# Starting every SBUF tile of a two-layer decoder trunk on a multiple of 256 bytes

## The chip, the cores and the metric

The kernel runs on one core of one Trainium2 chip. Times are device microseconds of one execution of the whole program; the number compared is the median of several executions. Before the change three executions gave 946.52, 948.52 and 952.02 us, median 948.52 us.

TensorE (PE) multiplies a stationary operand of at most 128x128 with a moving operand of up to 512 columns and writes to PSUM. The load of the stationary operand is an instruction of its own in the trace, LDWEIGHTS, shown as engine PEld. VectorE (DVE), ScalarE (ACT) and GpSimd (POOL) do the elementwise work, and SyncE (SP) issues every DMA here. SBUF has 128 partitions; an address below is a byte offset inside a partition, the same in all of them.

## The reference

A causal trunk of two layers on 512 tokens of 1024 features, all in float32:

```
for i in range(2):
    hn = rms_norm(h, norm_mix[i])
    h += pooling_mixer(hn)  if i == 0  else  sliding_window_attention(hn)
    hn = rms_norm(h, norm_ffn[i])
    u = hn @ w_in                      # 1024 -> 2 * 2816
    c = causal_depthwise_conv(u, width 3) + conv_b
    a, g = split(c)
    h += (a * silu(g)) @ w_out         # 2816 -> 1024
out = rms_norm(h, norm_f)
```

The pooling mixer takes windowed means (2, 4, 8, 16 tokens) minus the token and multiplies each group of 256 features with its own matrix. The attention has 16 query heads on 4 key heads, a window of 128, a bias by distance and one sink per head.

## The kernel before

Activations lie feature-major, 128 features by 512 tokens in a tile of 2048 bytes per partition. A float32 product is made of three passes: each operand is split into a high and a low float32r part, and `mm3` (lines 78 to 82) issues high x high, low x high and high x low, with a weight slice of 128 columns stationary and the activations moving. So nearly all of PE's work is a stream of matmuls with 512 moving columns, each with its own weight load.

In order of time:

- Pooling mixer, line 252: `xt` against the band matrices (line 267), then `px` parts against `wpool` parts, 48 matmuls.
- MLP of layer 0, lines 371 to 375: twice a half of the input projection (`mlp_in`, `f0x` parts against `wi` parts, 528 matmuls a half) and of the output projection (`mlp_out`, `zh`/`zl` against `wo`, 264 matmuls a half).
- Attention, lines 378 to 617: keys and queries (`ax` against `kq`), values (`wv` moving, `ax` stationary, 256 columns), then 16 units of scores (`kh`/`kl` against `q`, line 536), softmax, transposes (line 567) and weighted values (`th`/`tl` against `vh`/`vl`, 256 columns) with query and output projections filled in between, and the rest of the output projection (`oh`/`ol` against `wo`).
- MLP of layer 1, lines 621 to 657, as in layer 0 with `f1x`. The last output projection runs five of its eight chunks with 512 columns; the last three are done in two halves of 256 columns, one of them with its weights in the tiles named `wk`.

Weights come by DMA into `raw` tiles (line 86), ACT copies the high part (line 94) and DVE or POOL subtracts for the low part (line 95), a few tiles ahead of PE. The order on each engine is the order of the code, held together by semaphores.

Where a tile lies follows from the pools. Pools stand one behind the other in SBUF, and each tile in them takes its size rounded up to 32 bytes. A tile of one column takes 32 bytes, and everything behind it is shifted by that. The pool `cst` stands first, then `wp` (weights), `xp` (`h` and the parts of the normed activations), `sm` (small and shared tiles), and behind them one pool for each phase: `first`, `fp0`, `ap`, `fp1`.

Of the kernel before, what the change touches and what calls it, by code (L numbers as in the profile page):

```python
"""Two-layer hybrid decoder trunk (pooling mixer, sliding-window attention, gated conv MLPs).

Activations are kept feature-major, [feature (partition), chunk, token], so that every product has
a weight tile as its stationary and all 512 tokens as its moving operand, and the causal
convolution runs along the free dimension.

float32 products: each operand is split exactly into two float32r parts, x = h + l, and a product
is the three passes hh + hl + lh. The scale of an RMSNorm is per token: it is multiplied in after
the product that follows the norm.
"""  # L10
# [9 lines left out]
F32 = mybir.dt.float32  # L20
F32R = mybir.dt.float32r
I32 = mybir.dt.int32
AF = mybir.ActivationFunctionType
# [3 lines left out]
P = 128  # L27
D = 1024
S = 512
NC = D // P  # feature chunks  # L30
NT = S // P  # token tiles
WINDOWS = (2, 4, 8, 16)
BW = P + 16  # tokens that a token tile's windows reach
FF = 2816
NF = FF // P  # chunks of one half of the MLP's input projection
NFH = NF // 2
HD = 64
# [5 lines left out]
# Columns of the packed per-feature vectors.  # L43
# [10 lines left out]
NV = V_SINK + NH  # L54
# [3 lines left out]
def trunk(ctx: ExitStack, tc: tile.TileContext, x_tok, x_t, vecs, w_pool, w_kq, w_v, w_o, w_in, w_out, out_a, out_b):  # L58
# [9 lines left out]
    # The banks of PSUM, handed out round-robin within rings that each phase sets.  # L68
    pp = ctx.enter_context(tc.tile_pool(name="pp", bufs=1, space=PSUM))
    banks = [pp.tile([P, S], F32, name=f"bank{i}") for i in range(8)]  # L70
    rings = {}
# [17 lines left out]
    def weights(src, n, name, eng=None, raw=None):  # L89
        """[128, n] of a weight from DRAM, n <= 1024, as its two parts."""  # L90
        raw = raw or fetch(src, n, name)
        h = wp.tile([P, 1024], F32R, tag="wh", name=f"{name}_h")
        l = wp.tile([P, 1024], F32R, tag="wl", name=f"{name}_l")
        A.activation(h[:, :n], raw[:, :n], AF.Copy)  # L94
        (eng or V).tensor_tensor(l[:, :n], raw[:, :n], h[:, :n].bitcast(F32), ALU.subtract)  # L95
        return h, l
# [14 lines left out]
    def kept_weights(layer, half, m):  # L111
        """The same, in the tiles of the split activations, which are free by then."""
        res = []
        for a in range(0, NFH, 4):
            n = (min(a + 4, NFH) - a) * P
            raw = fetch(w_out[layer, half, m, :, a * P : a * P + n], n, f"wk{m}_{a}")
            h = xp.tile([P, S], F32R, tag="xh", name=f"wk{m}_{a}_h")
            l = xp.tile([P, S], F32R, tag="xl", name=f"wk{m}_{a}_l")
            A.activation(h[:, :n], raw[:, :n], AF.Copy)
            V.tensor_tensor(l[:, :n], raw[:, :n], h[:, :n].bitcast(F32), ALU.subtract)  # L120
            res += [part((h, l), k) for k in range(n // P)]
        return res

    eps = cst.tile([P, 1], F32, name="eps")
    V.memset(eps, EPS)

    def load_root(x, name):
        """Has the scalar engine load the square root's table ahead of its use."""
        A.activation(sm.tile([P, 1], F32, tag="root", name=name), x, AF.Sqrt)
# [9 lines left out]
    vec = cst.tile([P, NV], F32, name="vec")  # L139
# [13 lines left out]
    # Windowed mean minus identity, as [token, token it reaches], for inner tiles and the first.  # L153
    rc = fst.tile([P, 16], F32, name="rc")
# [18 lines left out]
    def rsqrt_mean(dst, ssq, n, root=False):  # L173
        """dst = (ssq / D + eps) ** -0.5 on [128, n], from an integer guess or from the scalar engine's square root."""

        def tmp(k, dt=F32):
            return sm.tile([P, NT], dt, tag=f"rs_{k}", name=f"rs_{k}", bufs=4)[:, :n]

        v = tmp("v")
        y = tmp("y")  # L180
        if root:
            A.activation(y, ssq, AF.Sqrt, bias=eps, scale=1.0 / D)
            V.tensor_scalar(v, ssq, -0.5 / D, -0.5 * EPS, ALU.mult, ALU.add)
            V.reciprocal(y, y)
        else:
            V.tensor_scalar(v, ssq, 1.0 / D, EPS, ALU.mult, ALU.add)
            sh = tmp("i", I32)
            V.tensor_scalar(sh, v.bitcast(I32), 1, None, ALU.logical_shift_right)
            V.tensor_scalar(y.bitcast(I32), sh, -1.0, float(0x5F3759DF), ALU.mult, ALU.add)
            V.tensor_scalar(v, v, -0.5, None, ALU.mult)  # L190
        t = tmp("t")
        steps = 1 if root else 3
        for it in range(steps):
            z = dst if it == steps - 1 else y
            if n == 1:
                V.scalar_tensor_tensor(t, y, y, v, ALU.mult, ALU.mult)
            else:
                V.tensor_tensor(t, y, y, ALU.mult)
                V.tensor_tensor(t, t, v, ALU.mult)
            V.scalar_tensor_tensor(z, t, 1.5, y, ALU.add, ALU.mult)  # L200

    class Norm:
        """Sums of squares of the chunks of h, then the scale of each token."""
# [17 lines left out]

        def stats(self, ps, tiles=range(NT)):
            """r[token, tile]."""
            n = len(tiles)
            for i, j in enumerate(tiles):
                T.matmul(ps[:, 2 * i : 2 * i + 2], lhsT=self.acc[:, j * P : (j + 1) * P], rhs=ones[:, :2], start=True, stop=True)  # L226
            r = sm.tile([P, NT], F32, tag="r", name=f"{self.name}_r")
            rsqrt_mean(r[:, :n], ps[:, : 2 * n].rearrange("p (a b) -> p a b", b=2)[:, :, 0], n)
            return r

        def spread(self, ps, r, tiles=range(NT)):
            """r broadcast over the partitions, [128, token]."""
# [10 lines left out]
    def split_scaled(src, g, name):  # L243
        """The parts of src * g, g per feature."""
        xh = xp.tile([P, S], F32R, tag="xh", name=f"{name}_h")
        xl = xp.tile([P, S], F32R, tag="xl", name=f"{name}_l")
        A.activation(xh, src, AF.Copy, scale=g)  # L247
        V.scalar_tensor_tensor(xl, src, g, xh.bitcast(F32), ALU.mult, ALU.subtract)  # L248
        return xh, xl

    # ================= layer 0: pooling mixer =================
    def pool_mixer(norm, xs, ws):
        r0 = fst.tile([P, NT], F32, name="r0")
        ss0 = fst.tile([P, NT], F32, name="ss0")
                # The tensor engine's clock rises only after some microseconds of products.
        warm = fst.tile([P, BW], F32, name="warm")
# [35 lines left out]
        bs = cst.tile([P, NC], F32, name="bs")  # L292
# [12 lines left out]
    # ================= gated MLP with causal depthwise convolution =================  # L305
    def conv_chunk(fp, layer, ps, rb, m, name):
        """The convolution of chunk m of the input projection."""
# [9 lines left out]
    def mlp_in(fp, layer, half, xs, norm, rb, ws0=None):  # L317
        """Half of the hidden features, as chunks of parts. Without rb, the norm is finished on the way."""
# [58 lines left out]
    # ================= layer 1: sliding-window attention =================  # L377
    rings.update(t=[6, 7], s=[2, 3, 4], pj=[5, 0], av=[1])
    with tc.tile_pool(name="ap", bufs=2) as ap:
        # dist[q, j] = j - 128 - q for key j of [previous block, block], where query q sees it.  # L380
# [4 lines left out]
        # Queries are scaled by HD**-0.5 / slope, and the scores with their distances by slope.  # L385
        slopes = [2.0 ** (-8.0 / NH * (i + 1)) for i in range(NH)]
        qs = ap.tile([P, NC], F32, name="qs", bufs=1)
        for i in range(NH):
            G.memset(qs[(i % 2) * HD : (i % 2 + 1) * HD, i // 2 : i // 2 + 1], HD**-0.5 / slopes[i])
        bqs = ap.tile([P, NC], F32, name="bqs", bufs=1)  # L390
        V.tensor_tensor(bqs, vec[:, V_BQKV : V_BQKV + 8], qs, ALU.mult)

        # Values, [token, zero | head 0 | zero | head 1 | ... | zero].
# [11 lines left out]
        # Keys and values.  # L405
# [25 lines left out]
        def keys(n):  # L431
            """The parts of a head's keys, each in both halves of the partitions."""
# [11 lines left out]
        def queries(c, ps):  # L444
            """Per head of a chunk of queries, its high part in its half of the partitions and its low part in the other."""
# [26 lines left out]
        # Work for the tensor engine between the stages of the attention.  # L472
# [24 lines left out]
        def work():  # L497
            """Yields after each step, once its operands are there, the units of attention that the next one needs."""
# [22 lines left out]
        def scores(n, b):  # L521
            w = P if b == 0 else 2 * P
            neg = ap.tile([P, 4], F32, tag="neg", name=f"neg{n}{b}", bufs=3)
            den = ap.tile([P, 4], F32, tag="den", name=f"den{n}{b}", bufs=3)
            es = ap.tile([P, 4], F32, tag="es", name=f"es{n}{b}", bufs=3)
# [63 lines left out]
        # A unit's scores, the transposes of the one two before, and the values of the one three before.  # L589
        RATE = 3.4  # steps of filling work per unit  # L590
# [28 lines left out]
    # ================= layer 1: MLP, then the last norm =================  # L619
    HS = S // 2  # L620
    with tc.tile_pool(name="fp1", bufs=2) as fp:
# [19 lines left out]
        def turn(m):  # L641
            """The second half of the tokens of a chunk, token-major."""
# [46 lines left out]
        r = sm.tile([P, NT], F32, tag="r", name="n3b_r")  # L689
# [72 lines left out]
```

## Time and profile before

| | |
|---|---|
| three executions | 946.52, 948.52, 952.02 us |
| span of the profiled execution | 950.6 us (the page gives no other time of it) |
| PE busy | 929.2 us, 98% |
| PEld busy | 775.0 us, 82% |
| DVE busy | 586.8 us, 62% |
| ACT busy | 426.6 us, 45% |
| POOL busy | 139.2 us, 15% |
| DMA, mean over the span | 93 GB/s |

A matmul is shown for longer than it keeps the next one off: the matmuls overlap in PE's pipeline, and each one's end is modelled. What a matmul costs in a stream is the distance between its start and the next one's, and that is read from the start times or from the count of matmuls in a stretch. A stretch counts every matmul that is shown in it, so also the one or two (0.39 us shown, one started every 0.23 us, so 1.7 on average) that had started before it.

### The profile page before, as it was taken

The numbers are of one execution on the slowest core, as the hardware profiler recorded it, in microseconds if no ns is written. First come the engines' busy times: TensorE is split into PE (matmuls) and PEld (weight loads), VectorE is DVE, ScalarE is ACT, GpSimd is POOL, SyncE is SP. The second block draws the span as 40 slices with busy tenths as digits, with TensorE's granted clock in tenths as the row PEclk, the third lists the DMA queues.
The fourth block names the chain that finished last, engine by engine and source line by source line (L and its number), as shares of the span: only waits on it lengthen the run. The fifth ranks groups of instructions, "written<-read, shape, count | busy, mean of one in ns | idle before, by whom it ended". The sixth has DMA issues, their size and how long they took to land.

```text
span 950.6 us, 11713 instructions
## 1 busy us (share of the span) xinstructions
PE 929.2 (98%) x4419; PEld 775.0 (82%) x4419; DVE 586.8 (62%) x974; ACT 426.6 (45%) x690; POOL 139.2 (15%) x203
## 2 busy tenths in 40 slices
PE   8999999999999999997999999999999999999997
PEld 7788888888888888885788888888888888888886
DVE  5689675336777654338888571897753367776433
ACT  7565443223444433226877551644432234444432
POOL 9500000000000001442654231000000000000013
PEclk9999999999999999997999999999999999999998
DMA  8133323332322233322101031332223332222322
GB/s 328 64 111 114 108 62 81 101 131 93 110 89 86 71 92 106 111 89 67 45 23 46 1 133 45 111 125 97 70 83 92 132 100 101 89 97 62 91 61 89
DMA packets 28855, 88.13 MB, mean 93 GB/s; under 512 B 3200, under 2 KB 4352, under 8 KB 28800
## 3 DMA queue, kind: packets, MB, share of 16 engines
q1 hardware_dynamic: 28800, 87.40, 28.3%
q8 instruction: 34, 0.56, 0.2%
q14 instruction: 21, 0.17, 0.1%
HBM read 85.29 MB, written 2.10 MB: 92 GB/s over the span
## 4 chain that ended last, share of the span: by engine, by line
PE 90%; DVE 5%; ACT 3%; POOL 1%; issue 1%; ACTq 0%; DVEq 0%; POOLq 0%
PE bank L80 29%; PE bank L81 29%; PE bank L82 29%; PE bank L536 1%; DVE q L455 1%; PE bank L567 1%; ACT sc L555 1%; DVE sc L539 1%; ACT px_h L247 0%; DVE tl L571 0%; DVE vl L468 0%; ACT wi_h L94 0%; PE bank L267 0%; DVE f0x_l L248 0%; PE bank L226 0%
## 5 line engine op out<-in xcount | busy, mean ns | idle before, releaser
L220 POOL TENSOR_TENSOR n_acc<-n_acc,n_sq 128x512 f32<-128x512 f32 (+1 forms) x28 | 39.6, 1414 | 720.4 <-ACT n_sq L211 713.6
L94 ACT ACTIVATE wi_h<-wi_raw 128x1024 fp32r<-128x1024 f32 x88 | 93.0, 1061 | 111.0 <-PE bank L81 101.8
L80 PE MATMUL bank<-zh,wo_h 128*128 128x512 f32 (+1 forms) x363 | 138.9, 383 | 0.0
L82 PE MATMUL bank<-zh,wo_l 128*128 128x512 f32 (+1 forms) x363 | 138.4, 381 | 0.0
L81 PE MATMUL bank<-zl,wo_h 128*128 128x512 f32 (+1 forms) x363 | 138.4, 381 | 0.0
L81 PE MATMUL bank<-f0x_l,wi_h 128*128 128x512 f32 x352 | 137.1, 389 | 0.5 <-DVE f0x_l L248 0.5
L80 PE MATMUL bank<-f0x_h,wi_h 128*128 128x512 f32 x352 | 137.2, 390 | 0.0
L80 PE MATMUL bank<-f1x_h,wi_h 128*128 128x512 f32 x352 | 137.1, 390 | 0.0
L82 PE MATMUL bank<-f0x_h,wi_l 128*128 128x512 f32 x352 | 137.0, 389 | 0.0
L82 PE MATMUL bank<-f1x_h,wi_l 128*128 128x512 f32 x352 | 137.0, 389 | 0.0
L81 PE MATMUL bank<-f1x_l,wi_h 128*128 128x512 f32 x352 | 136.9, 389 | 0.0
L95 DVE TENSOR_TENSOR wi_l<-wi_raw,wi_h 128x1024 fp32r<-128x1024 f32 x84 | 102.6, 1224 | 49.7 <-ACT wi_h L94 37.9
L94 ACT ACTIVATE wo_h<-wo_raw 128x768 fp32r<-128x768 f32 (+1 forms) x70 | 57.5, 823 | 129.4 <-PE bank L81 116.9
L309 DVE TENSOR_TENSOR c_u<-bank,n_rb 128x512 f32<-128x512 f32 x88 | 60.0, 687 | 75.6 <-PE bank L82 75.6
L95 DVE TENSOR_TENSOR wo_l<-wo_raw,wo_h 128x768 fp32r<-128x768 f32 (+1 forms) x66 | 60.4, 914 | 56.3 <-ACT wo_h L94 56.1
L82 PEld LDWEIGHTS bank<-zh,wo_l 128*128 128x128 f32 x363 | 68.2, 188 | 14.5
L81 PEld LDWEIGHTS bank<-zl,wo_h 128*128 128x128 f32 x363 | 68.2, 188 | 14.3
L80 PEld LDWEIGHTS bank<-zh,wo_h 128*128 128x128 f32 x363 | 68.2, 188 | 14.3
L81 PEld LDWEIGHTS bank<-f0x_l,wi_h 128*128 128x128 f32 x352 | 66.1, 188 | 14.4 <-DVE f0x_l L248 1.0
L80 PEld LDWEIGHTS bank<-f0x_h,wi_h 128*128 128x128 f32 x352 | 66.1, 188 | 14.1 <-DVE h L301 0.4
L312 ACT ACTIVATE c_t<-c_u,vec 128x512 f32<-128x512 f32 x88 | 70.6, 811 | 15.4 <-DVE c_u L309 14.5
L82 PEld LDWEIGHTS bank<-f1x_h,wi_l 128*128 128x128 f32 x352 | 66.1, 188 | 13.8
(173 smaller groups left out, 1515.9 us busy)
## 6 DMA issues: line engine op xcount, KB each, us to landing
wi_raw<-w_in SPq DMA_DIRECT2D x88, 512.0 KB, 3.2
wo_raw<-w_out SPq DMA_DIRECT2D x31, 384.0 KB, 3.1
wo_raw<-w_out SPq DMA_DIRECT2D x31, 320.0 KB, 2.9
kq_raw<-w_kq SPq DMA_DIRECT2D x10, 512.0 KB, 3.3
wo_raw<-w_o SPq DMA_DIRECT2D x8, 512.0 KB, 3.2
xt<-x_tok SPq DMA_DIRECT2D x4, 512.0 KB, 5.2
h<-x_t SPq DMA_DIRECT2D x8, 256.0 KB, 8.1
wpool_raw<-w_pool SPq DMA_DIRECT2D x2, 512.0 KB, 7.9
```

The costliest lines, as they stand in the source:

```text
L80: T.matmul(ps, lhsT=wh, rhs=xh, start=start, stop=False, **kw)
L81: T.matmul(ps, lhsT=wh, rhs=xl, start=False, stop=False, **kw)
L82: T.matmul(ps, lhsT=wl, rhs=xh, start=False, stop=stop, **kw)
L94: A.activation(h[:, :n], raw[:, :n], AF.Copy)
L95: (eng or V).tensor_tensor(l[:, :n], raw[:, :n], h[:, :n].bitcast(F32), ALU.subtract)
L220: eng.tensor_tensor(self.acc[:, lo:hi], self.acc[:, lo:hi], sq[:, lo:hi], ALU.add)
L309: V.tensor_tensor(u, ps, rb, ALU.mult)
L312: A.activation(t, u, AF.Identity, bias=col(V_CB + layer * 2 * NF + m), scale=cw[2])
L455: V.tensor_tensor(t[dst], u[src], t[src].bitcast(F32), ALU.subtract)
L536: T.matmul(o, lhsT=qt, rhs=kt[:, kk : kk + 256], start=x == 0, stop=x == 1)
L539: V.tensor_tensor_reduce(out=st[:, par, :w], in0=ps[:, par * 256 : par * 256 + w], in1=dist[:, 2 * P - w :], scale=slopes[4 * n + i], scal ...
L555: A.activation(t, t, AF.Exp, bias=neg[:, i : i + 1], accum_out=den[:, i : i + 1])
```

## The change

A helper `small` asks the pool for a tile of a given number of 32-bit words and returns its first columns. It is used for all tiles that are not already a multiple of 256 bytes, with sizes chosen so that the tiles behind them begin on a multiple of 256 bytes. Comments and docstrings are emptied, which shifts line numbers by a few. No instruction is added, taken away or moved on any engine, and no wait changes; operands keep their shapes. What differs is the address of nearly every tile. The end of the used SBUF moves from byte 226,176 to byte 228,096.

```
+    def small(pool, n, words, dt=F32, **kw):
+        return pool.tile([P, words], dt, **kw)[:, :n]
...
-    eps = cst.tile([P, 1], F32, name="eps")
+    eps = small(cst, 1, 32, name="eps")
...
-        A.activation(sm.tile([P, 1], F32, tag="root", name=name), x, AF.Sqrt)
+        A.activation(small(sm, 1, 32, tag="root", name=name), x, AF.Sqrt)
...
-    vec = cst.tile([P, NV], F32, name="vec")
+    vec = small(cst, NV, -(-NV // 64) * 64, name="vec")
...
-    rc = fst.tile([P, 16], F32, name="rc")
+    rc = small(fst, 16, 64, name="rc")
...
-            return sm.tile([P, NT], dt, tag=f"rs_{k}", name=f"rs_{k}", bufs=4)[:, :n]
+            return small(sm, n, 16, dt, tag=f"rs_{k}", name=f"rs_{k}", bufs=4)
...
-            r = sm.tile([P, NT], F32, tag="r", name=f"{self.name}_r")
+            r = small(sm, NT, 32, tag="r", name=f"{self.name}_r")
...
-        warm = fst.tile([P, BW], F32, name="warm")
+        warm = small(fst, BW, 192, name="warm")
...
-        bs = cst.tile([P, NC], F32, name="bs")
+        bs = small(cst, NC, 64, name="bs")
...
-        qs = ap.tile([P, NC], F32, name="qs", bufs=1)
+        qs = small(ap, NC, 32, name="qs", bufs=1)
...
-            neg = ap.tile([P, 4], F32, tag="neg", name=f"neg{n}{b}", bufs=3)
-            den = ap.tile([P, 4], F32, tag="den", name=f"den{n}{b}", bufs=3)
-            es = ap.tile([P, 4], F32, tag="es", name=f"es{n}{b}", bufs=3)
+            neg = small(ap, 4, 32, tag="neg", name=f"neg{n}{b}", bufs=3)
+            den = small(ap, 4, 16, tag="den", name=f"den{n}{b}", bufs=3)
+            es = small(ap, 4, 16, tag="es", name=f"es{n}{b}", bufs=3)
```

(`r0`, `ss0`, `bqs` and the last `r` are changed in the same way.)

The remainders of the tiles' addresses, as the two programs are built. The slices that PE takes of a float32r tile begin a multiple of 256 bytes into it, so a slice has its tile's remainder.

| tiles | address mod 256 before | after |
|---|---|---|
| weights in `wp` (`wi`, `wo`, `kq`, `wv`: raw, h, l) | 160 | 0 |
| `xp`: `h`, `px`, `f0x`, `ax`, `f1x`, `wk` | 160 | 0 |
| `zh`, `zl`, `c_u`, `c_t`, `zz`, `hg`, `xt` | 32 | 0 |
| `wpool` parts | 224 | 0 |
| `oh`, `ol`, `kh`, `kl`, `q`, `vh`, `vl`, `n_acc`, `n_sq` | 96 | 0 |
| `sc`, `th`, `tl`, `ident`, `ones` | 128 | 0 |

So before the change the two operands of a matmul have these remainders (moving, stationary): `f0x`, `f1x` and `ax` against `wi` and `kq` 160 and 160; `wv` against `ax` 160 and 160; `kh`, `kl` against `q` 96 and 96; `zh`, `zl` against `wo` or `wk` 32 and 160; `oh`, `ol` against `wo` 96 and 160; `px` against `wpool` 160 and 224; `th`, `tl` against `vh`, `vl` 128 and 96. After it all of them have 0 and 0.

## Rows read from the trace of the kernel before

**Rows 1.** The page: span, busy time of the engines, chain that ended last.
```profile
span 950.6 us, 11713 instructions
PE 929.2 (98%) x4419; PEld 775.0 (82%) x4419; DVE 586.8 (62%) x974; ACT 426.6 (45%) x690; POOL 139.2 (15%) x203
PE 90%; DVE 5%; ACT 3%; POOL 1%; issue 1%; ACTq 0%; DVEq 0%; POOLq 0%
```

**Rows 2.** Stretches: start:end, length, PE busy, instructions, granted clock, DMA.
```profile
60.00:150.00 90.00, 90.00 (x399) 1.00 0.29 94
152.00:212.00 60.00, 60.00 (x259) 1.00 0.34 105
334.00:393.00 59.00, 59.00 (x255) 1.00 0.35 106
440.00:480.00 40.00, 35.61 (x199) 0.91 0.16 54
480.00:520.00 40.00, 37.06 (x231) 0.96 0.11 40
```

**Rows 3.** Timeline of PE, input projection: start, shown length, engine, line, operands.
```profile
99.96 0.39 PE L80 MATMUL bank<-f0x_h,wi_h 128*128 128x512 f32 x1
...
102.91 0.39 PE L81 MATMUL bank<-f0x_l,wi_h 128*128 128x512 f32 x1
```

**Rows 4.** Timeline of PE, output projection of the MLP.
```profile
160.06 0.39 PE L80 MATMUL bank<-zh,wo_h 128*128 128x512 f32 x1
...
162.86 0.39 PE L80 MATMUL bank<-zh,wo_h 128*128 128x512 f32 x1
```

**Rows 5.** Timeline of PE, end of the attention's output projection.
```profile
570.17 0.39 PE L80 MATMUL bank<-oh,wo_h 128*128 128x512 f32 x1
...
574.84 0.39 PE L82 MATMUL bank<-oh,wo_l 128*128 128x512 f32 x1
```

**Rows 6.** Timeline of PE, products of the pooling mixer.
```profile
19.98 0.40 PE L80 MATMUL bank<-px_h,wpool_h 128*128 128x512 f32 x1
...
23.94 0.39 PE L82 MATMUL bank<-px_h,wpool_l 128*128 128x512 f32 x1
```

**Rows 7.** Timeline of PE, matmuls of 256 columns: values, then last output projection.
```profile
409.77 0.28 PE L80 MATMUL bank<-wv_h,ax_h 128*128 128x256 f32 x1
...
411.69 0.28 PE L81 MATMUL bank<-wv_l,ax_h 128*128 128x256 f32 x1
...
921.43 0.28 PE L81 MATMUL bank<-zl,wo_h 128*128 128x256 f32 x1
...
926.54 0.28 PE L82 MATMUL bank<-zh,wo_l 128*128 128x256 f32 x1
```

**Rows 8.** Groups by line and shape: count, busy, mean ns, idle before and releasers.
```profile
L80 PE MATMUL bank<-f0x_h,wi_h 128*128 128x512 f32 x352 | 137.2, 390 | 0.0
L80 PE MATMUL bank<-zh,wo_h 128*128 128x512 f32 x319 | 126.2, 396 | 0.0
L80 PE MATMUL bank<-oh,wo_h 128*128 128x512 f32 x64 | 25.5, 401 | 0.0
L80 PE MATMUL bank<-zh,wo_h 128*128 128x256 f32 x44 | 12.7, 288 | 0.0
L80 PE MATMUL bank<-zh,wk_h 128*128 128x256 f32 x22 | 6.3, 285 | 0.0
L94 ACT ACTIVATE wi_h<-wi_raw 128x1024 fp32r<-128x1024 f32 x88 | 93.0, 1061 | 111.0 <-PE bank L81 101.8 <-DMA wi_raw<-w_in 4.7 <-DVE rs_t L198 2.8
L309 DVE TENSOR_TENSOR c_u<-bank,n_rb 128x512 f32<-128x512 f32 x88 | 60.0, 687 | 75.6 <-PE bank L82 75.6
L571 DVE TENSOR_TENSOR tl<-bank,th 128x512 fp32r<-128x512 f32 x28 | 18.7, 684 | 1.8 <-ACT th L570 1.4
```

**Rows 9.** Timeline of PE, query projection inside the attention.
```profile
482.18 0.40 PE L81 MATMUL bank<-ax_l,kq_h 128*128 128x512 f32 x1
...
483.81 0.39 PE L82 MATMUL bank<-ax_h,kq_l 128*128 128x512 f32 x1
```

More of the change, by code (lines that the diff above doesn't have):

```diff
@@ L252, in pool_mixer @@
     def pool_mixer(norm, xs, ws):
-        r0 = fst.tile([P, NT], F32, name="r0")
-        ss0 = fst.tile([P, NT], F32, name="ss0")
-        warm = fst.tile([P, BW], F32, name="warm")
+        r0 = small(fst, NT, 32, name="r0")
+        ss0 = small(fst, NT, 32, name="ss0")
+        warm = small(fst, BW, 192, name="warm")
         V.memset(warm, 0.0)
@@ L386, in trunk @@
         slopes = [2.0 ** (-8.0 / NH * (i + 1)) for i in range(NH)]
-        qs = ap.tile([P, NC], F32, name="qs", bufs=1)
+        qs = small(ap, NC, 32, name="qs", bufs=1)
         for i in range(NH):
             G.memset(qs[(i % 2) * HD : (i % 2 + 1) * HD, i // 2 : i // 2 + 1], HD**-0.5 / slopes[i])
-        bqs = ap.tile([P, NC], F32, name="bqs", bufs=1)
+        bqs = small(ap, NC, 32, name="bqs", bufs=1)
         V.tensor_tensor(bqs, vec[:, V_BQKV : V_BQKV + 8], qs, ALU.mult)
@@ L688, in trunk @@
         turn(NC - 1)
-        r = sm.tile([P, NT], F32, tag="r", name="n3b_r")
+        r = small(sm, NT, 32, tag="r", name="n3b_r")
         for j in range(2):
```

## The prediction

> **What bounds the kernel now.** I read the page's busy times and the chain that ended last first, then the stretches, then PE's start times, then the groups by line. PE is busy for 929.2 of 950.6 us, and the chain is PE for 90% [rows 1]. [...]
>
> [...] All these matmuls have 128x128 weights and 512 moving columns. Input projection: 13 distances from 99.96 to 102.91 us, 2.95/13 = 226.9 ns [rows 3]. MLP output projection: 12 from 160.06 to 162.86, 2.80/12 = 233.3 ns [rows 4]. The stretches say the same with more counts: 90.00/(399 - 1.7) = 226.5 ns; 60.00/(259 - 1.7) = 233.2 ns; 59.00/(255 - 1.7) = 232.9 ns [rows 2]. The attention's output projection has 4.67/20 = 233.5 ns [rows 5], the pooling products 3.96/17 = 232.9 ns [rows 6].
>
> Beside the table of remainders in the section on the change, these fall into two classes. The stream at 226.6 ns has both operands at the same remainder (160 and 160). The three at 233 ns have different ones (32 and 160; 96 and 160; 160 and 224). No engine, DMA or clock separates them: the stretches of both kinds have clock 1.00 and DMA shares of 0.29 to 0.35 [rows 2]. I take it that a matmul's stream and the weight load running beside it disturb each other a little when their lines are out of step, some 6.6 ns for each matmul. After the change all are in step.
>
> **The change part by part.** No instruction, order or wait changes, so every term is a distance.
>
> 1. `zh`, `zl` against `wo`, 512 columns: 3 passes x 319 = 957 matmuls [rows 8], each from 233.2 to 226.6 ns: 957 x 6.6 = 6.3 us, all in stretches where PE has no idle time. What would be late next is the weights, and they have room: ACT's splits of the input weights stood 101.8 of 111.0 us waiting for PE to give a tile back and 4.7 us for DMA [rows 8]. PE asking 3% sooner does not use that up.
>
> 2. `oh`, `ol` against `wo`: 3 x 64 = 192 matmuls [rows 8]. By the code 36 of them (two chunks, six steps each) fill gaps of the attention, where PE is not the bound; 156 stand behind it. 156 x (233.5 - 226.6) = 1.1 us.
>
> 3. `px` against `wpool`, 48 matmuls at 232.9 ns: at most 0.3 us. They run next to a chain through ACT and DVE that delivers the normed activations for the first MLP, which PE then waits for; I count nothing.
>
> 4. 256 columns. In step, `wv` against `ax` has 1.92/16 = 120.0 ns; out of step, `zh` and `zl` have 5.11/43 = 118.8 ns [rows 7]. Here being in step costs 1.2 ns. The last three output chunks have 3 x (44 + 22) = 198 of these [rows 8]: 0.2 us lost.
>
> 5. The attention. PE is idle for 4.4 and 2.9 us in two stretches of 40 us, with the clock at 0.91 and 0.96 [rows 2], so the softmax's chain has a part in the end there. Its `ax` against `kq` matmuls are in step already and still have 1.63/7 = 232.9 ns [rows 9]: they come in bursts between other kinds, and a burst seems to need some matmuls before it settles. So I expect nothing from `th`/`tl`, which become in step, and take 0, between -1 us (the 36 + 168 + some projection matmuls gaining) and +1 us (168 `th`/`tl` matmuls paying the 1.2 ns of term 4 and a moved wait).
>
> 6. Everything else. DVE's 512-column subtraction into `tl` (remainder 128) takes 684 ns, the one into `c_u` (remainder 32) 687 ns [rows 8]: elementwise instructions don't see the start address. For DMA into aligned tiles the trace has no row, since no big tile is at 0 now. A gain there is hidden for the reason in term 1; a loss would have to exceed the tiles fetched ahead. I take 0 for both. At the very start, where the first loads could matter, the chain is POOL's work on the band matrices, the 1% of POOL in it [rows 1].
>
> Sum against the profiled execution: 950.6 - 6.3 - 1.1 + 0.2 = 943.4 us, -0.76%. The profiled span stands inside the three timed executions (946.52 to 952.02) and 0.2% above their median, so on the median 948.52 x 943.4/950.6 = 941.3; I say 941.5 us. Its own range is 938 to 945: 2.5 us for the attention, whose waits and clock dips can land otherwise, and as much for the run-to-run spread of 5.5 us among three.
>
> [...]
>
> **The rivals.**
>
> No change: the 6.6 ns belong to something else that the output projections have, such as weights taken from tiles of 768 and 640 columns. For it: the in-step burst at 232.9 ns in the attention [rows 9], and that I know of no row with the same tiles at other addresses. Against it: `px` and `oh` share neither weights' shape nor phase with `zh`, and have the same 233. It gives 948.5 us.
>
> Larger gain: every tile before starts 32 past a multiple of 64, `sc`, `th`, `tl`, `ident` and `ones` excepted, and 226.6 ns may itself hold a cost of that start. [...]
>
> [...]
>
> Slower: not equality settles the stream at 226.6 ns but the remainder 160 of both operands, and with both at 0 their first lines meet. Then the 2,112 input-projection matmuls go at the 233.2 ns that the rest has, 2,112 x 6.6 = 13.9 us, and the output projections gain nothing: 948.5 + 13.9 = 962.4 us. For it: only remainder 160 has a long settled stream in the trace, and rows 9 show that equality alone does not bring it at once. Against it: nothing in the rows singles out 160. It decides as soon as the stretch from 60 to 150 us holds 388 matmuls in place of 399.
>
> **How the numbers follow.** Forecast 0.72, larger gain 0.11, no change 0.10, slower 0.07. A measurement of this kernel can tell about 0.5% (4.7 us) from no change. The forecast's 0.76% lies a little beyond that, so of its 0.72 I give 0.59 to faster and 0.13 to within; with the larger gain faster is 0.70, with the no-change case (0.09 within, 0.01 slower) same is 0.22, and slower 0.08. The range: 938 to 945 holds nearly all of the forecast, 0.70. Up to 950 it takes most of the no-change case, and down to 925 a mild form of the larger gain (6 ns off each of 3,225 matmuls would be 922): together about 0.8.
>
> **What would show it.** Right: starts in the MLP output projection 226.7 ns apart, so a stretch of 60 us inside it holds 266 matmuls and not 259; the attention's output projection likewise; the input projection as now, at 399 in 90 us; the last halves at 120.0 ns; DVE's 687 ns and ACT's 1061 ns unmoved; PE's idle time about 21 us as before. Term 1 is wrong if the output projection stays at 233. The forecast as a whole is wrong if the input projection moves, in either direction, or if the part between the values and the attention's output projection [rows 7, 5] changes its length by more than 2 us beside term 2.

## The result, and the profile after

The changed kernel takes 944.09 us (median of 6 executions, 940.98 to 944.51) against 950.08 us for the kernel before, run on the same chip (6 executions, 946.52 to 952.32). The ratio is 0.9931, 95% interval [0.9908, 0.9955]: 0.7% faster, clear of the interval and a little beyond the 0.5% set ahead. Forecast were 941.5 us from a median of 948.52, a ratio of 0.9926.

One thing is needed to read the smaller differences below: the executions of each of these kernels fall on two levels some 3 to 5 us apart (on the lower one lay three of the six of the kernel before here, one of the 17 and one of the 11 that the experiments are compared with, and five of the twelve of the experiment called "z moved back"), so where a term of about 1 us is at stake I compare medians of the upper level within one set of runs.

The page of the kernel after has the span, the busy times and the chain; they answer to [rows 1].

```profile
span 942.7 us, 11713 instructions
PE 919.2 (97%) x4419; PEld 773.1 (82%) x4419; DVE 587.2 (62%) x974; ACT 426.5 (45%) x690; POOL 138.9 (15%) x203
PE 90%; DVE 5%; ACT 3%; POOL 1%; issue 1%; ACTq 0%; DVEq 0%; POOLq 0%
```

The span is 7.9 us shorter, and PE's busy time fell by 10.0 us with the same 4419 matmuls; PE's idle time grew from 21.4 to 23.5 us. DVE, ACT and POOL have the busy times of before to within 0.5 us. So what changed is on PE alone. Stretches of the kernel after, with the columns of [rows 2]; the third begins 1 us earlier than its counterpart, inside the same output projection:

```profile
60.00:150.00 90.00, 90.00 (x399) 1.00 0.29 93
152.00:212.00 60.00, 60.00 (x267) 1.00 0.36 112
333.00:392.00 59.00, 59.00 (x262) 1.00 0.37 115
```

The input projection has 399 matmuls in 90 us as before. The output projection has 267 and 262 where it had 259 and 255.

Timeline of PE in the kernel after: output projection of the MLP, end of the attention's output projection, and the last halves of 256 columns; they answer to [rows 4, 5, 7]. Line 80 of before is line 84 here.

```profile
159.80 0.39 PE L84 MATMUL bank<-zh,wo_h 128*128 128x512 f32 x1
...
162.98 0.39 PE L86 MATMUL bank<-zh,wo_l 128*128 128x512 f32 x1
...
563.69 0.39 PE L84 MATMUL bank<-oh,wo_h 128*128 128x512 f32 x1
...
569.58 0.39 PE L86 MATMUL bank<-oh,wo_l 128*128 128x512 f32 x1
...
913.57 0.28 PE L85 MATMUL bank<-zl,wo_h 128*128 128x256 f32 x1
...
919.56 0.28 PE L84 MATMUL bank<-zh,wo_h 128*128 128x256 f32 x1
```

These are 14, 26 and 50 distances: 3.18/14 = 227.1, 5.89/26 = 226.5 and 5.99/50 = 119.8 ns. Before they were 233.3, 233.5 and 118.8. Over all 957 matmuls of 512 columns in the MLP output projections the distances add up to 217.3 us, and to 223.4 before.

Groups of the kernel after, which answer to [rows 8]:

```profile
L98 ACT ACTIVATE wi_h<-wi_raw 128x1024 fp32r<-128x1024 f32 x88 | 93.0, 1061 | 109.3 <-PE bank L85 102.4 <-DMA wi_raw<-w_in 4.1 <-DVE rs_t L202 2.8
L313 DVE TENSOR_TENSOR c_u<-bank,n_rb 128x512 f32<-128x512 f32 x88 | 60.1, 688 | 76.2 <-PE bank L86 76.2
```

DVE's instruction into `c_u` and ACT's split of the weights have the durations of before (687 and 1061 ns): their tiles moved, from 32 and 160 past a multiple of 256 to 0, and they did not notice.

### The profile page after: what moved, and what is told of

It is laid out like the page before. It is cut to its first block, busy times and chain, and to the rows that moved or that the text cites. A ratio compares the mean times of both kernels' runs of the same rounds, so it can differ in the third digit from the quotient of the medians.

```text
span 942.7 us, 11713 instructions
## 1 busy us (share of the span) xinstructions
PE 919.2 (97%) x4419; PEld 773.1 (82%) x4419; DVE 587.2 (62%) x974; ACT 426.5 (45%) x690; POOL 138.9 (15%) x203
## 4 chain that ended last, share of the span: by engine, by line
PE 90%; DVE 5%; ACT 3%; POOL 1%; issue 1%; ACTq 0%; DVEq 0%; POOLq 0%
PE bank L85 29%; PE bank L84 29%; PE bank L86 29%; PE bank L540 1%; DVE q L459 1%; PE bank L571 1%; ACT sc L559 1%; DVE sc L543 1%; ACT px_h L251 0%; DVE tl L575 0%; DVE vl L472 0%; ACT wi_h L98 0%; PE bank L271 0%; DVE f0x_l L252 0%; PE bank L230 0%
## 5 line engine op out<-in xcount | busy, mean ns | idle before, releaser
L98 ACT ACTIVATE wi_h<-wi_raw 128x1024 fp32r<-128x1024 f32 x88 | 93.0, 1061 | 109.3 <-PE bank L85 102.4
L84 PE MATMUL bank<-zh,wo_h 128*128 128x512 f32 (+1 forms) x363 | 137.0, 378 | 0.0
```

What stands on the lines that cost most here:

```text
L84: T.matmul(ps, lhsT=wh, rhs=xh, start=start, stop=False, **kw)
```

## The experiments

Two questions were open after this. Is it the difference between the two starts that counts, or that both lie on a multiple of 256? And do the terms of the sum have the sizes given to them? Four kernels move groups of tiles by one unused tile at the head of a pool; two run bare streams of matmuls.

**One pad.** The kernel before, with

```
+        V.memset(fp.tile([P, 32], F32, name="pad", bufs=1), 0.0)
```

at the head of the pools `fp0` and `fp1`. It moves every tile of these two pools by 128 bytes, also `c_u`, `c_t`, `zz` and `hg`; of them only `zh` and `zl` are operands of PE's long streams.

> The kernel before, with one unused tile of 128 bytes at the head of the two MLP pools, so that zh and zl start 160 past a multiple of 256, like the weights they meet; all else has the addresses of before, and nothing starts on a multiple of 256. Theory (only the difference of the two starts counts): the MLP output projection falls from 233.3 to 226.7 ns, 957 matmuls give back 6.1 us, the 198 of 256 columns cost 0.2 us; about 0.9937 of before. Rival (a start on a multiple of 256 is what helps): the output projection stays at 233.3 ns and the time at 1.000 of before.

Measured: 945.17 us, ratio to before 0.9928 [0.9914, 0.9942]. A stretch of this kernel in the first output projection:

```profile
152.00:212.00 60.00, 60.00 (x266) 1.00 0.36 111
```

It holds 266 matmuls; the kernel after has 267 there, the kernel before 259 [rows 2]. No large tile of this kernel lies on a multiple of 256, so the rival is out: at 160 and 160 the stream is as fast as at 0 and 0. On the upper level the median went from 951.35 to 945.24 us, 6.1 us, which is term 1 less the 0.2 us of term 4.

**z moved back.** The kernel after with the same line at the head of the same pools, which puts `zh`, `zl` and the other tiles of these pools at 128 and leaves the rest at 0.

> The kernel after, with one unused tile of 128 bytes at the head of the two MLP pools, so that zh and zl start 128 past a multiple of 256 and everything else on one. Theory: the MLP output projection is back at 233.3 ns and 6 us of the 7 are lost, 0.9993 of before; the attention's output projection stays at 226.7 ns. Rival (the rest of the alignment carries the gain): it keeps most of it, 0.994.

Measured: 950.09 us, ratio 0.9974 [0.9960, 0.9987]. The same stretch:

```profile
152.00:212.00 60.00, 60.00 (x259) 1.00 0.34 105
```

259, exactly the count of before. That ratio is of all executions and lower than the 0.9993 expected; on the upper level it is 950.38 against 951.35 us, 0.9990: 1.0 us is left of 7, about what term 2 should leave. All of the gain but that hangs on where the z tiles lie against the weights. DVE's instruction into `c_u`, which moved along with them, kept its 687 ns.

**Everything 32 bytes further.** The kernel after, with

```
-    eps = small(cst, 1, 32, name="eps")
+    eps = small(cst, 1, 40, name="eps")
```

> The kernel after, with the first small tile 32 bytes longer, so that every large tile starts 32 past a multiple of 256, all at the same remainder. Theory (only the difference counts): all streams at 226.7 ns as in the kernel after, 0.993 of before. Rival (a start on a multiple of 256 is what helps): the output projections go back to 233 ns, 1.000 of before; a second rival, that a remainder other than 0 or 160 does not settle at 226.7 ns at all, gives 1.015.

Measured: 944.24 us, ratio 0.9920 [0.9905, 0.9935]; on the upper level 944.27 against 951.35 us, 7.1 us, the whole predicted gain. The stretch from 60 to 150 us:

```profile
60.00:150.00 90.00, 90.00 (x399) 1.00 0.29 92
```

So the multiple of 256 in the description of the change is not what matters, and the prediction's slower rival, that a common start other than 160 might not settle, is out for 32 as well as for 0.

**Streams.** A kernel of matmuls alone:

```
for i in range(60):
    T.matmul(bank, lhsT=st[:, s // 4 + 128 * (i % 4) :][:, :128],
             rhs=mv[i % 2][:, m // 4 :][:, :n], start=i == 0, stop=i == 59)
```

with `mv` and `st` on multiples of 256 and m, s the bytes of the start in them.

> Computes nothing of the reference: 23 streams of 60 matmuls each, with weight loads, that differ in where the moving and the stationary operand start. float32r, 512 columns, stationary at 0: theory 226.7 ns between starts with the moving operand at 0 or 256, 233 ns at 32, 64, 96, 128, 160, 192, 224; equal starts of 128, 16 or 4 again 226.7; the stationary at 128 and the moving at 0 233. Rival: equal starts of 128, 16 or 4 are at 233 too. At 16 and 4 against 0 the theory says 233 if every difference counts, 226.7 if only whole steps of 32 do. [...] bfloat16 with 512 columns, an open question: 213 to 227, with a difference between 0 and 128 if the weight load is what gets in the way.

Its timeline merges each stream of 60 into one row: start, shown length, line. The distance is the next row's start less the row's own, over 60. In order m, s: L46 64, 0; L50 128, 0; L62 128, 128; L64 16, 16; L66 4, 4; L68 0, 128; L70 256, 0; L72 and L74 256 columns and L76 and L78 384 columns, each at 0, 0 and 128, 0; L80 and L82 bfloat16 at 0, 0 and 128, 0.

```profile
38.02 13.91 PE L46 MATMUL bank<-mv,st 128*128 128x512 f32 x60
51.76 14.17 PE L48 MATMUL bank<-mv,st 128*128 128x512 f32 x60
65.77 14.16 PE L50 MATMUL bank<-mv,st 128*128 128x512 f32 x60
79.77 14.21 PE L52 MATMUL bank<-mv,st 128*128 128x512 f32 x60
...
149.91 13.78 PE L62 MATMUL bank<-mv,st 128*128 128x512 f32 x60
163.52 14.03 PE L64 MATMUL bank<-mv,st 128*128 128x512 f32 x60
177.39 14.43 PE L66 MATMUL bank<-mv,st 128*128 128x512 f32 x60
191.65 14.11 PE L68 MATMUL bank<-mv,st 128*128 128x512 f32 x60
205.60 13.77 PE L70 MATMUL bank<-mv,st 128*128 128x512 f32 x60
219.20 7.36 PE L72 MATMUL bank<-mv,st 128*128 128x256 f32 x60
226.39 7.29 PE L74 MATMUL bank<-mv,st 128*128 128x256 f32 x60
233.51 10.57 PE L76 MATMUL bank<-mv,st 128*128 128x384 f32 x60
243.92 10.72 PE L78 MATMUL bank<-mv,st 128*128 128x384 f32 x60
254.48 13.13 PE L80 MATMUL bank<-mvb,stb 128*128 128x512 bf16 x60
267.44 13.11 PE L82 MATMUL bank<-mvb,stb 128*128 128x512 bf16 x60
280.39 13.11 PE L84 MATMUL bank<-mvb,stb 128*128 128x512 bf16 x60
```

The reader is to see: 226.8 ns at 128, 128 (149.91 to 163.52) and 226.7 at 256, 0; 233.3 at 128, 0 and 232.5 at 0, 128. That is the theory, without any other engine at work. Two things are not. A difference of 64 costs only 229.0 ns. And equal starts of 16 and of 4 are at 231.2 and 237.7 ns, so to be equal is not enough; the theory's 226.7 for them was wrong. With the stationary operand at 0, moving starts of 16 and 4 have 231.7 and 236.5 ns, close to the equal starts: below a step of 32 bytes it is not equality that decides. 256 columns give 119.8 and 118.7 ns, close to the 120.0 and 118.8 of [rows 7], 384 columns 173.5 and 176.0 ns. bfloat16 has 216.0 and 215.8 ns and does not care.

**Two pads.** One pad, and 64 bytes at the head of the attention's pool (`ap.tile([P, 16], ...)`), which puts `oh` and `ol` at 160 too. This run and the next two were made on another chip than the first four, with executions of the kernel before on that chip beside them.

> The kernel before with two unused tiles: 128 bytes at the head of the two MLP pools and 64 bytes at the head of the attention's pool, so that zh, zl, oh and ol start 160 past a multiple of 256, like the weights they meet. px against wpool stays out of step, and so do th, tl against vh, vl (192 and 160). Theory (the output projections are the whole gain): the 1.1 us that the first pad alone left out comes on top of it, the time of the kernel after to within 0.3 us, 0.9920 to 0.9930 of before on the same chip, with the attention's output projection at 226.7 ns. Rival (the aligned small tiles, the pooling products or the attention's operands carry a part): it stays 0.5 to 1.5 us behind the kernel after.

Measured: 944.54 us, ratio 0.9921 [0.9909, 0.9934]; on the upper level 944.55 against 951.27 us, 6.7 us. A stretch of the attention's output projection in one pad (first row) and in two pads (second):

```profile
540.00:565.00 25.00, 25.00 (x109) 1.00 0.39 127
```
```profile
540.00:565.00 25.00, 25.00 (x112) 1.00 0.39 127
```

The stream went to its faster pace, 25/(112 - 1.7) = 226.7 ns. The two pads, two lines, give 6.7 of the 7.1 us that the common shift gives against the same kernel before. The remaining 0.4 us is less than medians from two chips can tell; the profiled spans of two pads and of the kernel after are 942.8 and 942.7 us.

**The attention's pool moved back.** The kernel after with 96 bytes at the head of `ap`, so that its tiles lie at 96.

> The kernel after, with one unused tile of 96 bytes at the head of the attention's pool, so that all of the attention's own tiles start 96 past a multiple of 256 and the weights on one: oh, ol against wo out of step, all others in step. Theory: the attention's output projection back at 233 ns, 1.1 us of the 7 lost, 0.1% slower than the kernel after. Rival (the attention loses by its new addresses what the oh term gives): no difference from the kernel after.

Measured: 944.02 us, ratio 0.9912 [0.9896, 0.9929]; on the upper level 944.52 against 951.27 us, 6.7 us where 6.0 were expected. Its stretch from 540 to 565 us:

```profile
540.00:565.00 25.00, 25.00 (x109) 1.00 0.46 148
```

`oh` against `wo` is back at 233 ns, so 1 us was lost there as the theory says, and some 0.7 us came back elsewhere. I take that to be the attention, whose other operands are in step in both kernels, but it is not shown: this kernel's profile is of an execution of 940.0 us, 4.5 us below that median, and the kernel after was not run beside it on this chip. The rival, that the execution shows no loss, is not excluded. This run is inconclusive for term 5.

**Streams with narrower weights.** The same loop with `lhsT` of 128, 96, 64 and 32 columns, more starts, the kernel's order of three passes, and bursts of six matmuls of 512 columns and four of 256.

> Computes nothing of the reference: 18 streams of 60 float32r matmuls with 512 moving columns. [...] Stationary at 192 with the moving at 0, the same difference as 64 against 0 in the first set: 228.9 ns if only the difference counts; stationary at 32 and 64: 233. Equal starts of 32 and 64: 226.7; of 8: 231 to 238, like 16 and 4. The three passes in the kernel's own order: 226.7 in step, 233.3 out of step. Six matmuls of 512 columns and four of 256 by turns: if a stream needs time to settle, in step 229 to 231 ns for the 512s and no gain over out of step; if not, 226.7 and 120.

Timeline; L41, L43, L45 have 96, 64 and 32 weight columns at 0, 0, and L47, L49, L51, L53 128, 96, 64 and 32 at 128, 0; L57 0, 64; L59 0, 192; L61 8, 8; L63 32, 32; L65 64, 64; L67 and L69 the three passes in step and 128 out.

```profile
24.57 13.97 PE L41 MATMUL bank<-mv,st 128*96 128x512 f32 x60
38.38 13.96 PE L43 MATMUL bank<-mv,st 128*64 128x512 f32 x60
52.17 14.07 PE L45 MATMUL bank<-mv,st 128*32 128x512 f32 x60
66.07 14.10 PE L47 MATMUL bank<-mv,st 128*128 128x512 f32 x60
80.01 14.06 PE L49 MATMUL bank<-mv,st 128*96 128x512 f32 x60
93.91 13.93 PE L51 MATMUL bank<-mv,st 128*64 128x512 f32 x60
107.67 14.00 PE L53 MATMUL bank<-mv,st 128*32 128x512 f32 x60
121.51 14.15 PE L55 MATMUL bank<-mv,st 128*128 128x512 f32 x60
135.50 14.16 PE L57 MATMUL bank<-mv,st 128*128 128x512 f32 x60
149.50 13.91 PE L59 MATMUL bank<-mv,st 128*128 128x512 f32 x60
163.25 14.15 PE L61 MATMUL bank<-mv,st 128*128 128x512 f32 x60
177.24 13.79 PE L63 MATMUL bank<-mv,st 128*128 128x512 f32 x60
190.87 13.79 PE L65 MATMUL bank<-mv,st 128*128 128x512 f32 x60
204.49 13.78 PE L67 MATMUL bank<-mv,st 128*128 128x512 f32 x60
218.11 14.15 PE L69 MATMUL bank<-mv,st 128*128 128x512 f32 x60
232.10 11.31 PE L72 MATMUL bank<-mv,st 128*128 128x512 f32 x60
```

0, 192 has 229.2 ns, like 64, 0, and 0, 64 has 233.3: between starts on multiples of 32, what counts is their difference, taken modulo 256, with its sign. Equal starts of 32 and 64 have 227.2 and 227.0 ns, the first few matmuls of each stream included, equal starts of 8 have 233.2. The three passes have 227.0 and 233.2 ns. In the bursts, in step, the six distances of the 512s were 233, 236, 228, 233, 231 and 226 ns in each of the last rounds, 231 on average: in step, a stream of float32r matmuls takes some matmuls to reach its pace, which is what [rows 9] showed. Out of step the six had 232.8 or 233.7 on average, the pace of a long stream out of step, so in bursts being in step gains some 2 ns and not 6.6. And the distance did not shrink with the weights' width. In step it was 230.2, 229.8 and 231.7 ns for 96, 64 and 32 columns, where 128 have 227.0, although the weight loads themselves became shorter, 188, 161, 134 and 109 ns for 128, 96, 64 and 32 columns. Out of step the four widths have 232.3, 231.7, 229.3 and 230.7 ns: with 64 or 32 weight columns being in step gains nothing. The idea behind this run, that reading the weights takes the moving operand's place, byte for byte, by which narrower weights would go faster in step, has fallen, and that of the same cost for every width with it.

## Why the prediction was right

- The bound. Right: in the MLP stretches PE is busy without a gap at a granted clock of 1.00 in both kernels (90.00 of 90.00 us, 60.00 of 60.00, 59.00 of 59.00), so the time there is the number of matmuls times the distance between their starts, and a shorter distance there came out at the end of the kernel undiminished.
- Term 1, 6.3 us. The distances of the 957 matmuls add up to 6.1 us less, and one pad, which changes terms 1 and 4 alone, gave 6.1 us net. The counts were predicted as 266 in 60 us; 267 were there. Weights were not late: ACT's wait for a free tile stayed at 102 us.
- Term 2, 1.1 us. The distances of all 192 matmuls add up to 44.5 us and 45.6 before, 1.1 us; in executions two pads showed 0.6 us more than one pad, on another chip and at the edge of what medians resolve.
- Term 3, nothing on the path. Right for the reason given: the 48 matmuls ran 0.3 us shorter, and PE's next wait for DVE's `f0x_l` grew by as much. The waits of PE on that instruction, before and after:

```profile
PE bank L81 <- DVE f0x_l L248: 0.5, 1, 0.5
```
```profile
PE bank L85 <- DVE f0x_l L252: 0.8, 1, 0.8
```

- Term 4, 0.2 us lost. The 198 distances went from 23.9 to 24.1 us.
- Term 5, 0 within 1 us either way. In the profiled executions the attention from the end of the values to its first uninterrupted `oh` matmul is 0.8 us shorter, 115.7 against 116.5. That this comes from addresses is not shown: one pad, with the attention's addresses of before, has 115.1. What goes with it is the clock. Stretches that hold this part, in the kernel before, the kernel after and one pad:

```profile
416.00:533.00 117.00, 106.05 (x606) 0.94 0.13 46
```
```profile
412.00:528.00 116.00, 103.81 (x608) 0.96 0.13 46
```
```profile
412.00:528.00 116.00, 105.14 (x609) 0.96 0.14 46
```

The kernel before was granted 0.94 there, the other two 0.96. So the 0.8 us goes with a clock dip that landed otherwise, which the range allowed for; no run shows any of it to come from operands in step.

- Sum. 943.4 us predicted for the profiled execution, 942.7 measured, and most of the 0.7 us is term 5. For the median 941.5 us was forecast and 944.09 measured: the step from the profiled execution to the median was off. In the kernel after, the execution of 944.47 us has a span of 942.7, so a span is some 1.8 us less than its time, and the profiled 950.6 us stood at the upper end of the three executions, not 0.2% above their median. The base, 948.52 us from three, became 950.08 from six; the ratio came out as 0.9931 for the 0.9926 forecast.
- A sign that did not come as said: PE's idle time was to stay at about 21 us and was 23.5. The waits that grew are those for `q` in the attention, 3.9 to 5.2 us, and for `rs_y` at the start, 1.1 to 1.9 us. The first is not the addresses' doing: z moved back, with the attention's addresses of the kernel after, has 3.9 us. The second cost nothing: the pooling products behind it start at 17.1 us in both kernels.
- The rivals. No change and larger gain went out with the first profile, since the output projections moved to 226.7 ns and the input projections stayed. No run shows the 6 ns off each of 3,225 matmuls (2,112 of the input projections, 957 and 156) that the range holds for a mild form of the larger gain: with all starts at 0, and with all at 32, the input projection kept its 399 matmuls in 90 us, 226.5 ns. The slower one, that 160 is special, went out with it too: 399 matmuls from 60 to 150 us and not 388.
- The reason behind it, that stream and weight load disturb each other when out of step, is only half shown. That the distance follows the difference of the two starts modulo 256 is shown by one pad, the common shift and the streams, for starts on multiples of 32 and 128 weight columns. The streams, with no other engine at work, show 226.7 to 237.7 ns by start address alone, so the two operands of a matmul do concern each other. Why the pace in step is 226.7 ns, where the bfloat16 streams have 215.8 and 216.0, and what meets what, stays open after the narrower weights.

## What to carry to other kernels

When the same shape of matmul has two paces in one trace (226.6 and 233 ns here) and PE never idles in either, look up where the operands lie before looking for waits. For float32r with 128 weight columns and 512 moving columns, let the two operands begin at the same remainder modulo 256, on a multiple of 32 (0, 32, 64, 128 and 160 were run, with 226.5 to 227.2 ns); one unused tile in front of a pool does that (6.1 of the 7.1 us here, 6.7 with two), and aligning every tile is not needed. Do it where long streams run: in bursts of six it gained some 2 ns (231 against 233). Matmuls of 256 moving columns lose 1 ns by it (119.8 against 118.7), and 64 or 32 weight columns (229.8 and 231.7 ns in step, 229.3 and 230.7 out of it) and bfloat16 (216.0 and 215.8) gain nothing.

## What the runs showed of the hardware

- Distances between float32r matmuls with 128 weight columns and 512 moving columns at a granted clock of 1.00 (0.993 on the mean in the second set of streams), by start of the moving and the stationary operand modulo 256: equal multiples of 32 (0, 32, 64, 128 in the streams) 226.7 to 227.2 ns; 64 more on the moving side 229.0; other differences in multiples of 32 232.3 to 234.2; equal 16 231.2, equal 8 233.2, equal 4 237.7.
- At the lower clock the distance goes with the columns. Pieces of the chain in the kernel before, from 433.6 to 436.6 us, at a granted clock of 0.55 (0.50 for nearly all of it), are 0.43 us each. From 444.84 to 449.53 us, at 0.50, the same kind of matmul, with 512 columns, has 4.69/11 = 426.4 ns, 0.83 ns a column. These are in step (160 and 160). Matmuls of 256 columns have as much for a column there, in step and out of it: at a granted clock of 0.50 `th` and `tl` against `vh` and `vl` started 0.85/4 = 212.5 ns apart in the kernel after (0 and 0), from 492.97 to 493.82 us, and 213 to 214 ns apart in one pad (128 and 96), from 492.27 to 493.55 us. At 1.00 a column takes 0.44 ns in 512 (226.6 ns, in step) and 0.46 to 0.47 in 256 (118.7 to 120.0 ns).

```profile
434.63 0.43 PE bank L80
435.06 0.43 PE bank L81
```

- The attention's length goes with the clock that it is granted. From the end of the values to the first uninterrupted `oh` matmul it takes 116.5 us in the kernel before, at a clock of 0.94; 114.9 to 115.8 us in five kernels at 0.96, whatever their addresses; and 110.6 us in the last pool experiment, at 0.97:

```profile
412.00:523.00 111.00, 102.81 (x606) 0.97 0.14 48
```

Which of the two leads, and what sets the clock there, was not tried.
